# Seven block products per weight pair: another order of the products in gate and up, and another place for one of their PSUM tiles

## The chip, the cores and the metric

The kernel runs on one core of one Trainium2 chip. The metric is the device time of one execution in microseconds (us); lower is better. Engines are called by the names of the profile: PE (TensorE matmul), PEld (its weight load), DVE (VectorE), ACT (ScalarE), POOL (GpSimd), SP (SyncE, which here issues the loads).

## The reference

A trunk of two layers on 512 tokens with 1024 features: a gated short convolution first, then dilated attention, and behind each of them the same feed-forward block. The change lies in that block alone, in the two products `gate` and `up` (1024 features in, 2816 out, each):

```python
def swiglu(x, w_gate_up, w_down):
    g, u = jnp.split(x @ w_gate_up, 2, axis=-1)
    return (jax.nn.silu(g) * u) @ w_down

# once per layer:
f = swiglu(rms_norm(h, ffn_norm_pre[layer]), ffn_w_gate_up[layer], ffn_w_down[layer])
h = h + rms_norm(f, ffn_norm_post[layer])
```

All of it is float32. The kernel keeps each operand as a high part and a low part and adds three matmuls (high x high, low weights x high, high x low) for every block.

## The kernel before

**The stage.** `ffn` (L512) works through the gate and up columns in chunks of 256. Chunks 0 and 1 go through ordinary products. Chunks 2 to 10 (L543) go through the class `Pair` (L395): for each chunk one pair object for the gate columns, then one for the up columns, so 18 pairs per layer and 36 in the program. In what follows pair m is the m-th of a layer, from 0; even pairs are gates, odd ones are ups.

**One pair** multiplies 256 columns of weights (two blocks `n1`, `n2` of 128 columns, each in two halves `k1`, `k2` of the 1024 input features) by 512 tokens, and does it with seven block products in place of eight, on sums of the weight blocks and on sums of the token blocks (`xs`, made once per layer). A block product (L429) is 12 matmuls of 128x256. They are issued through `strict` (L134), which ties every matmul behind the one traced before, so PE runs the products in exactly the order in which `ffn` calls p1 to p7.

**The weights of a pair** are made when the object is built (L404 to L422), ahead of its first product: `a1` is the split of `n1` (ACT casts the high part, L94, DVE subtracts for the low part, L95); `dh` and `dl` (called `a22`) are the split of one quarter of the raw weights; then four additions on DVE (L407) overwrite the raw weights in place; then `s1` and `s2` are the splits of the two sums. Products 1 and 2 read `a1`, 6 and 3 read `s1`, 7 and 5 read `s2`, 4 reads `dh` and `dl`. `dh` and `dl` lie in the tag "ah" of the pool `apool`, which has 4 buffers: room for two pairs. `a1`, `s1` and `s2` share a tag of 6 buffers, the raw weights have 2.

**The results.** Three PSUM tiles per pair: `z` takes products 1, 6, 7 and 4 one after the other, each added onto the sum so far; `zx` takes product 2; `zy` takes 5 and later 3. PSUM has two tags, "mm" and "at", of 4 banks each. After each product on `z` the sum so far is read out before the next may be added: ACT copies it after p1 (L440) and after p6 (L448) and negates it after p7 (L455); after p4 ACT (gate, L471) or DVE (up, L473) reads it. DVE adds `zx` after p2 (L444), `zy` after p3 (L478); `c22` (L458 and L462 or L464) finishes the block that needs p7 and p5. p4 and p3 of a pair are held back and run between products of the next pair (`before` in L542 to L568).

**Everything else** on ACT, DVE and SP is placed by the tile planner when the program is built, instruction by instruction into one fixed queue per engine; a tile whose buffer is taken waits until the last reader of the tile before it is done. After the last pair the stage `down` (L343) follows, whose matmuls aren't tied to the order of the products.

Of the kernel before, what the change touches and what calls it, by code (L numbers as in the profile page):

```python
# [38 lines left out]
def trunk(  # L39
# [49 lines left out]
    def bank(tag, name):  # L89
        return psum.tile([P, T], F32, tag=tag, name=name)  # L90

    def split(hi, lo, src):

        return [nc.scalar.copy(hi, src).ins,  # L94
                nc.vector.tensor_tensor(lo, src, hi.bitcast(F32), ALU.subtract).ins]  # L95
# [9 lines left out]
    def parts(src, gain=None, pool=wp, bufs=6):  # L105


        _, a, b = src.shape
        w = pool.tile([P, 2 * a, b], F32R, tag="w", name="w", bufs=bufs, align_bytes=LINE)
        wh, wl = w[:, 0:a], w[:, a:2 * a]  # L110
        if gain is None:
            split(wh, wl, src)
            return wh, wl
        for i in range(a):
            g = gain[:, i:i + 1]
            nc.scalar.mul(wh[:, i], src[:, i], g)  # L116
            nc.vector.scalar_tensor_tensor(  # L117
                wl[:, i], src[:, i], g, wh[:, i].bitcast(F32), ALU.mult, ALU.subtract)
        return wh, wl
# [5 lines left out]
    def load_cols(w, c0):  # L125

        return load(w[:, c0:c0 + 256].rearrange("(k p) n -> p k n", p=P), KT, 256)
# [70 lines left out]
    def makers(tag, raw, gain=None, fused=True):  # L198

        ws = []  # L200

        def make(j):
            cs = slice(j * P, (j + 1) * P)
            ps = bank(tag, tag + "f")
            if gain is not None and not fused:
                for k in range(0, KT, 4):
                    g = gain[:, k:k + 4].rearrange("p (a x) -> p a x", x=1)
                    nc.vector.tensor_tensor(raw[:, k:k + 4, cs], raw[:, k:k + 4, cs],
                                            g.broadcast_to([P, 4, P]), ALU.mult)
            if gain is None or not fused:  # L210
                w = parts(raw[:, :, cs])
                return ps, lambda low, k: w[low][:, k, :]
            if not ws:
                ws.extend(gained(raw, gain))
            return ps, lambda low, k: ws[k // 4][low][:, k % 4, cs]

        return [lambda j=j: make(j) for j in range(2)]
# [76 lines left out]
    class Next:  # L294
# [3 lines left out]
        def __init__(self, pool, ys, gpost, gpre, n=0):  # L298
            self.pool, self.ys, self.n = pool, ys, n
            self.gpost, self.gpre = (g if g is None else row_gain(pool, g) for g in (gpost, gpre))  # L300
            self.hn, self.ssq, self.yg = {}, {}, {}
            self.marks, self.added, self.normed, self.made = {}, {}, {}, {}
# [92 lines left out]
    class Pair:  # L395
# [5 lines left out]
        def __init__(self, pool, raw, xs, gate, act):  # L401
            self.pool, self.xs, self.gate, self.act = pool, xs, gate, act
            n1, n2 = raw[:, :, 0:P], raw[:, :, P:2 * P]
            k1, k2 = slice(0, KT // 2), slice(KT // 2, KT)  # L404

            def add(out, a, b):
                nc.vector.tensor_tensor(out, a, b, ALU.add)  # L407

            a1 = parts(n1)
            a22 = [pool.tile([P, KT // 2, P], F32R, tag="ah", name=n, align_bytes=LINE)  # L410
                   for n in ("dh", "dl")]
            split(*a22, n2[:, k2])
            add(n2[:, k2], n2[:, k1], n2[:, k2])
            add(n2[:, k1], n1[:, k1], n2[:, k1])
            add(n1[:, k1], n1[:, k1], n2[:, k2])
            add(n1[:, k2], n1[:, k2], n1[:, k1])
            s1 = parts(n1)
            s2 = parts(n2)
            self.w = {
                1: [z[:, k1] for z in a1], 2: [z[:, k2] for z in a1],  # L420
                6: [z[:, k1] for z in s1], 3: [z[:, k2] for z in s1],
                7: [z[:, k1] for z in s2], 5: [z[:, k2] for z in s2], 4: a22}  # L422

            self.z, self.x, self.y = (bank(t, n)[:, 0:T // 2] for t, n in (
                ("mm", "z"), ("mm", "zx"), ("at", "zy")))
            self.r = pool.tile([P, T], F32, tag="al", name="r", align_bytes=LINE)
            self.r2 = pool.tile([P, T], F32, tag="al", name="r2", align_bytes=LINE)[:, 0:T // 2]

# [83 lines left out]
    def ffn(layer, pending, norms, after):  # L512
        w = ffn_w_gate_up[layer]
        with ExitStack() as phase:
            apool = phase.enter_context(tc.tile_pool(name=f"a{layer}", bufs=4))
            act = []
            for n, bufs in ((1, NF // 2 - 6), (0, 6)):
                actp = tc.tile_pool(name=f"act{layer}{n}", bufs=1)
                stack = phase.enter_context(ExitStack())
                pool = stack.enter_context(actp)  # L520
                act = [pool.tile([P, 2 * T], F32, tag=f"act{k}", name="act")
                       for k in range(bufs)] + act

            def loads(c):
                return [load_cols(w, c0 + c * 256) for c0 in (0, DFF)]

            for c in range(2):
                rg, ru = loads(c)
                mg, mu = makers("mm", rg), makers("at", ru)
                rest = pending.rest() if c == 0 else {}  # L530
                if c == 1:
                    rest["marks"] = [pending.made[NT - 1]] * 4
                ps = feature_mms([mg[0], mu[0], mg[1], mu[1]], **rest)
                for j in range(2):
                    s = apool.tile([P, T], F32, tag="silu", name="s", bufs=2)
                    nc.scalar.activation(s, ps[2 * j], AF.Silu)
                    nc.vector.tensor_tensor(
                        act[c][:, j * T:(j + 1) * T], ps[2 * j + 1], s, ALU.mult)
            norms.close()
            with tc.tile_pool(name=f"sums{layer}", bufs=1, side="right") as sums:  # L540
                xs = sums_of_x(sums, act[-4:])
                before = None  # L542
                for c in range(2, NF // 2):  # L543
                    gate = None
                    for raw in loads(c):
                        p = Pair(apool, raw, xs, gate, act[c])
                        p.p1()
                        if gate and c == NF // 2 - 1:
                            before.p4()
                            p.p6()  # L550
                            before.p3()
                            p.p7()
                            p.p2()
                            p.p5()
                            p.c22()
                            p.p4()
                            p.p3()
                            break
                        p.p2()
                        if before:  # L560
                            before.p4()
                        p.p6()
                        if before:
                            before.p3()
                        p.p5()
                        p.p7()
                        p.c22()
                        before = gate = p  # L568
            npool = norm_pool(norms, f"{layer}f")

            def held_pool():

                stack.close()
                return stack.enter_context(tc.tile_pool(name=f"held{layer}", bufs=2))

            halves = [a[:, j * T:(j + 1) * T] for a in act for j in range(2)]
            return down(apool, halves, ffn_w_down[layer], held_pool, lambda ys: after(npool, ys))

    def norm_pool(stack, n):

        return stack.enter_context(tc.tile_pool(name=f"norm{n}", bufs=2, side="right"))
# [3 lines left out]
    with ExitStack() as phase:  # L585
# [57 lines left out]
        for c in range(KT // 2):  # L643
# [56 lines left out]
            lambda: phase.enter_context(tc.tile_pool(name="heldc", bufs=2)),  # L700
            lambda ys: Next(npool, ys, mix_norm_post[0], ffn_norm_pre[0]))
    pending = ffn(0, pending, norm0, lambda pool, ys: Next(pool, ys, ffn_norm_post[0], None))


# [300 lines left out]
    with ExitStack() as phase:  # L1005
# [22 lines left out]
        class Last(Next):  # L1028
# [3 lines left out]
            def after_half(self, tt, n):  # L1032
                self.add(tt, n)
                if n == 1:
                    for q, c in zip((nc.sync, nc.scalar if tt == NT - 1 else nc.sync, nc.sync),
                                    self.pieces(tt)):
                        q.dma_start(out[0, tt * P:(tt + 1) * P, c], h[:, tt, c])

        ffn(1, pending, norm1, lambda pool, ys: Last(pool, ys, ffn_norm_post[1], None))


# [43 lines left out]
```

## Time and profile before

| | |
|---|---|
| time, median of 3 runs | 1454.47 us (1453.3 to 1454.65) |
| the profiled execution's own time | 1453.27 us |
| its span, first to last instruction | 1451.5 us |
| PE busy | 1433.4 us, 99% of the span |
| PEld / DVE / ACT / POOL busy | 1286.6 / 913.6 / 760.4 / 59.7 us |
| granted TensorE clock, mean | 0.997 |
| matmuls of the pairs (lines z, zx, zy of the page's part 5) | 864 + 432 + 432 in the lines shown, and those of p4 |

The busy time of PE is made of matmul records that overlap: a 128x256 matmul is recorded with 284 ns, while the next one starts 120 ns later. Progress is therefore read from starts, not from durations. A row of a timeline merges neighbouring instructions of one kind and gives the start, the time from the first start to the last end, and how many they are; a bracket says how long the engine was idle ahead of it and what ended that.

### The profile page before, as it was taken

Reading aid. Unit: us, or ns where it says so; the run is one execution under the profiler, and the core shown is the slowest. Engines: PE = TensorE matmul, PEld = TensorE weight load, DVE = VectorE, ACT = ScalarE, POOL = GpSimd, SP = SyncE. Lnnn points to the kernel's source line nnn. Section 1 sums busy time; section 2 is a strip of 40 time slices with the busy share of each in tenths; the row PEclk is TensorE's granted clock in tenths of the full one; section 3 lists DMA queues with packets and bytes.
Section 4 is the critical chain, followed back from the end, with each engine's and each line's share of the span. In section 5 each row is a group of like instructions: output and inputs, shape, how many; then the busy total and the mean of one; then the engine's idle time right before and its main releaser. Section 6 shows DMA issues by size and latency. Waiting matters only on the chain.

```text
span 1451.5 us, 23433 instructions
## 1 busy us (share of the span) xinstructions
PE 1433.4 (99%) x9456; PEld 1286.6 (89%) x9456; DVE 913.6 (63%) x1747; ACT 760.4 (52%) x1543; POOL 59.7 (4%) x108
## 2 busy tenths in 40 slices
PE   9999999999999999999999999999999999999998
PEld 7888898999988889898899889889789999998886
DVE  5644577888864456757457555755539688886433
ACT  5322344445443336896777778668544445454321
POOL 1000110000000010010000001000011000000000
PEclk9999999999999999999999999999999999999999
DMA  6333213232342402323212322321112232334311
GB/s 220 116 116 104 71 59 117 88 117 93 112 160 89 143 30 88 116 62 100 92 44 89 103 72 61 103 72 60 60 59 94 81 117 88 117 113 146 105 58 58
DMA packets 110530, 137.65 MB, mean 95 GB/s; under 512 B 3501, under 2 KB 99285, under 8 KB 110422
## 3 DMA queue, kind: packets, MB, share of 16 engines
q1 hardware_dynamic: 108852, 135.69, 28.2%
q8 instruction: 74, 1.21, 0.4%
q0 software_dynamic: 1280, 0.26, 0.3%
q14 instruction: 34, 0.28, 0.1%
q10 hardware_dynamic: 290, 0.20, 0.0%
HBM read 133.92 MB, written 2.23 MB: 94 GB/s over the span
## 4 chain that ended last, share of the span: by engine, by line
PE 95%; issue 2%; ACT 1%; DVE 1%; POOL 1%; POOLq 0%; DVEq 0%; ACTq 0%
PE mmf L134 17%; PE z L134 14%; PE vps L134 10%; PE atf L161 10%; PE zy L134 7%; PE mmf L161 7%; PE zx L134 4%; PE s L134 2%; PE o L134 2%; PE tr L134 2%; PE y L134 1%; PE tr L284 1%; PE y0a L230 1%; PE y1b L232 1%; PE y0a L232 1%
## 5 line engine op out<-in xcount | busy, mean ns | idle before, releaser
L95 DVE TENSOR_TENSOR w<-raw,w 128x1024 fp32r<-128x1024 f32 x212 | 251.6, 1220 | 81.7 <-ACT w L94 81.4
L94 ACT CAST w<-raw 128x1024 fp32r<-128x1024 f32 x212 | 212.7, 1046 | 107.3 <-PE atf L161 43.1
L134 PE MATMUL mmf<-x,w 128*128 128x512 f32 x1056 | 246.5, 391 | 0.0
L134 PEld LDWEIGHTS mmf<-x,w 128*128 128x128 f32 x1056 | 196.2, 188 | 39.4
L117 DVE SCALAR_TENSOR_TENSOR w<-raw,cols,w 128x256 fp32r<-128x256 f32 x272 | 115.4, 479 | 103.8 <-ACT w L116 103.8
L161 PE MATMUL atf<-x,w 128*128 128x512 f32 (+1 forms) x816 | 174.7, 340 | 0.0
L161 PEld LDWEIGHTS atf<-x,w 128*128 128x128 f32 x816 | 134.9, 190 | 16.8
L116 ACT ACTIVATE w<-raw,cols 128x256 fp32r<-128x256 f32 x272 | 115.1, 499 | 63.4 <-PE mmf L134 46.4
L134 PE MATMUL vps<-w,x 128*128 128x256 f32 x1152 | 142.3, 284 | 0.0
L134 PEld LDWEIGHTS vps<-w,x 128*128 128x128 f32 x1152 | 139.0, 192 | 1.9
L161 PE MATMUL mmf<-x,w 128*128 128x256 f32 (+1 forms) x624 | 131.3, 326 | 1.0 <-ACT x L94 0.6
L134 PE MATMUL z<-xs,w 128*128 128x256 f32 x864 | 115.8, 284 | 4.0 <-ACT r L440 4.0
L134 PEld LDWEIGHTS z<-xs,w 128*128 128x128 f32 x864 | 108.8, 192 | 4.6 <-ACT r L440 4.4
L161 PEld LDWEIGHTS mmf<-x,w 128*128 128x128 f32 x624 | 99.3, 191 | 11.5 <-ACT x L94 1.3
L407 DVE TENSOR_TENSOR raw<-raw 128x512 f32<-128x512 f32 x144 | 98.4, 688 | 2.9
L95 DVE TENSOR_TENSOR al<-act,ah 128x512 fp32r<-128x512 f32 x44 | 30.0, 690 | 90.1 <-ACT ah L94 90.0
L94 ACT CAST ah<-act 128x512 fp32r<-128x512 f32 x44 | 26.9, 620 | 110.2 <-PE y3b L230 101.7
L758 ACT COPY sw<-mmf 32x512 f32<-32x512 f32 x92 | 53.2, 578 | 30.1 <-PE mmf L134 18.8
L831 ACT ACTIVATE p<-p,nm 128x256 f32<-128x256 f32 (+1 forms) x128 | 61.5, 482 | 9.8 <-DVE nm L828 9.7
L760 DVE TENSOR_TENSOR qk<-mmf,cos 128x512 f32<-128x512 f32 x46 | 31.8, 690 | 46.4 <-ACT sw L759 46.3
L134 PE MATMUL zy<-xs,w 128*128 128x256 f32 x432 | 57.7, 283 | 0.0
L134 PE MATMUL zx<-x,w 128*128 128x256 f32 x432 | 57.7, 283 | 0.0
(220 smaller groups left out, 2403.7 us busy)
## 6 DMA issues: line engine op xcount, KB each, us to landing
raw<-in_ffn_w_gate_up SPq DMA_DIRECT2D x44, 1024.0 KB, 5.1
raw<-in_w_kv SPq DMA_DIRECT2D x24, 1024.0 KB, 5.2
raw<-in_ffn_w_down SPq DMA_DIRECT2D x22, 1024.0 KB, 4.9
raw<-in_w_q SPq DMA_DIRECT2D x12, 1024.0 KB, 5.0
raw<-in_conv_w_in SPq DMA_DIRECT2D x11, 1024.0 KB, 5.3
raw<-in_conv_w_out SPq DMA_DIRECT2D x4, 1024.0 KB, 4.9
raw<-in_w_o SPq DMA_DIRECT2D x4, 1024.0 KB, 5.1
h<-in_x SPq DMA_DIRECT2D x4, 512.0 KB, 7.3
```

The costliest lines, as they stand in the source:

```text
L94: return [nc.scalar.copy(hi, src).ins, nc.vector.tensor_tensor(lo, src, hi.bitcast(F32), ALU.subtract).ins]
L95: nc.vector.tensor_tensor(lo, src, hi.bitcast(F32), ALU.subtract).ins]
L116: nc.scalar.mul(wh[:, i], src[:, i], g)
L117: nc.vector.scalar_tensor_tensor(wl[:, i], src[:, i], g, wh[:, i].bitcast(F32), ALU.mult, ALU.subtract)
L134: traced[:] = [op(*args, **kwargs).ins]
L161: nc.tensor.matmul(*args, **kwargs)
L230: nc.tensor.matmul(o, ah, wl[i], start=False, stop=False)
L232: mm = nc.tensor.matmul(o, al, wh[i], start=False, stop=last)
L407: nc.vector.tensor_tensor(out, a, b, ALU.add)
L758: nc.scalar.copy(w[s:s + 32], y[s + 32:s + 64])
L760: nc.vector.tensor_tensor(d, y, co, ALU.mult)
L831: nc.scalar.activation(p, p, AF.Exp, bias=nm[:, b:b + 1], scale=0.125, accum_out=st[:, b, hh, 1:2])
```

## The change

Two edits in `Pair` and `ffn`. `zx` moves from the PSUM tag "mm" to "at", so that "mm" serves one tile per pair and "at" two. And the products come in another order. With n for the pair being built and b for the pair before it, the order from the second pair on was

p1(n), p2(n), p4(b), p6(n), p3(b), p5(n), p7(n), and c22(n) behind it;

it becomes

p1(n), p7(b), and c22(b) behind it, p2(n), p5(n), p6(n), p4(b), p3(b).

The last pair of a layer has its own order: p1, p4(b), p6, p3(b), p7, p2, p5, c22, p4, p3 becomes p1, p7(b), c22(b), p2, p6, p4(b), p5, p7, c22, p3(b), p4, p3. The number of products, matmuls, copies, additions, splits and loads stays as it was.

```diff
             self.z, self.x, self.y = (bank(t, n)[:, 0:T // 2] for t, n in (
-                ("mm", "z"), ("mm", "zx"), ("at", "zy")))
+                ("mm", "z"), ("at", "zx"), ("at", "zy")))
...
                         p.p1()
                         if gate and c == NF // 2 - 1:
+                            before.p7()
+                            before.c22()
+                            p.p2()
+                            p.p6()
                             before.p4()
-                            p.p6()
+                            p.p5()
+                            p.p7()
+                            p.c22()
                             before.p3()
-                            p.p7()
-                            p.p2()
-                            p.p5()
-                            p.c22()
                             p.p4()
                             p.p3()
                             break
+                        if before:
+                            before.p7()
+                            before.c22()
                         p.p2()
+                        p.p5()
+                        p.p6()
                         if before:
                             before.p4()
-                        p.p6()
-                        if before:
                             before.p3()
-                        p.p5()
-                        p.p7()
-                        p.c22()
                         before = gate = p
```

## Rows read from the trace of the kernel before

**Rows 1.** Waits of PE over the whole span: us, times, longest.
```profile
PE z L134 <- ACT r L440: 4.0, 2, 2.0
```

**Rows 2.** ACT's and PE's timelines at the last pair of the first layer.
```profile
409.20 3.87 ACT L94 CAST w<-raw 128x1024 fp32r<-128x1024 f32 x4
...
413.29 0.36 ACT L440 COPY r<-z 128x256 f32<-128x256 f32 x1
...
413.70 1.70 PE L134 MATMUL z<-xs,w 128*128 128x256 f32 x12 [2.01 <-ACT r L440]
```

**Rows 3.** Windows: us; busy PE, PEld, DVE, ACT, POOL; clock; DMA; GB/s.
```profile
257.46:267.54 10.08, 10.08 (x87) 10.08 (x85) 9.13 (x14) 3.58 (x7) 0.00 (x0) 1.00 0.31 104
267.54:277.62 10.08, 10.08 (x87) 10.08 (x85) 7.86 (x11) 6.54 (x11) 0.00 (x0) 1.00 0.32 106
```

**Rows 4.** PE's timeline from pair 2's p1 on (p1, p6, p3, p5, p7, p6).
```profile
257.46 1.60 PE L134 MATMUL z<-x,w 128*128 128x256 f32 x12
...
261.78 1.60 PE L134 MATMUL z<-xs,w 128*128 128x256 f32 x12
263.22 1.60 PE L134 MATMUL zy<-x,w 128*128 128x256 f32 x12
264.66 1.60 PE L134 MATMUL zy<-xs,w 128*128 128x256 f32 x12
266.10 1.60 PE L134 MATMUL z<-xs,w 128*128 128x256 f32 x12
...
271.86 1.60 PE L134 MATMUL z<-xs,w 128*128 128x256 f32 x12
```

**Rows 5.** Tile dh: what ended idle time before its instructions; us, times.
```profile
  PE z L134: 37.3, 31
```

**Rows 6.** ACT's timeline, weights of pairs 3 and 4.
```profile
261.86 0.62 ACT L94 CAST dh<-raw 128x512 fp32r<-128x512 f32 x1 [1.81 <-PE z L134]
...
267.80 0.39 ACT L455 ACTIVATE r<-z 128x256 f32<-128x256 f32 x1 [4.01 <-PE z L134]
268.08 2.94 ACT L94 CAST w<-raw 128x1024 fp32r<-128x1024 f32 x3
...
271.94 0.62 ACT L94 CAST dh<-raw 128x512 fp32r<-128x512 f32 x1 [0.35 <-PE z L134]
...
276.78 2.95 ACT L94 CAST w<-raw 128x1024 fp32r<-128x1024 f32 x3 [0.75 <-DVE raw L407]
```

**Rows 7.** DVE's timeline, weights of pair 3 and, from 272.56 on, of pair 4.
```profile
262.65 0.69 DVE L95 TENSOR_TENSOR dl<-raw,dh 128x512 fp32r<-128x512 f32 x1
263.37 1.42 DVE L407 TENSOR_TENSOR raw<-raw 128x512 f32<-128x512 f32 x2
...
265.80 0.68 DVE L484 TENSOR_TENSOR act<-r,s 128x512 f32<-128x512 f32 x1
266.40 0.69 DVE L407 TENSOR_TENSOR raw<-raw 128x512 f32<-128x512 f32 x1
...
269.15 3.50 DVE L95 TENSOR_TENSOR w<-raw,w 128x1024 fp32r<-128x1024 f32 x3 [0.51 <-ACT w L94]
272.56 0.42 DVE L444 TENSOR_TENSOR r<-zx,r 128x256 f32<-128x256 f32 x1
272.90 0.68 DVE L95 TENSOR_TENSOR dl<-raw,dh 128x512 fp32r<-128x512 f32 x1
273.61 1.42 DVE L407 TENSOR_TENSOR raw<-raw 128x512 f32<-128x512 f32 x2
...
275.28 1.41 DVE L407 TENSOR_TENSOR raw<-raw 128x512 f32<-128x512 f32 x2
277.86 3.50 DVE L95 TENSOR_TENSOR w<-raw,w 128x1024 fp32r<-128x1024 f32 x3 [1.17 <-ACT w L94]
```

**Rows 8.** Page, part 5: busy us, mean ns of one; idle before, releaser.
```profile
L95 DVE TENSOR_TENSOR w<-raw,w 128x1024 fp32r<-128x1024 f32 x212 | 251.6, 1220 | 81.7 <-ACT w L94 81.4
```

**Rows 9.** Window around the stall of rows 2; columns as in rows 3.
```profile
409.00:415.00 6.00, 3.99 (x34) 3.79 (x32) 5.06 (x5) 5.96 (x10) 0.00 (x0) 1.00 0.21 46
```

## The prediction

> **What bounds the kernel now.** I read the list of PE's waits first, then timelines and windows of the stage that the change touches. In the whole span PE waited for a copy of `z` only twice, 2.0 us each [rows 1]: once per layer, ahead of p6 of the last pair [rows 2]. In the two periods shown PE was busy for all of the 10.08 us [rows 3], and its seven products start 1.44 us apart (261.78, 263.22, 264.66, 266.10 in [rows 4]). So two products between two on one bank already hide the copies everywhere but at the end. PE is the bound of the stage; DVE comes next with 9.13 and 7.86 us of 10.08 [rows 3], and the reader should keep that closeness in mind.
>
> The second thing to see is how the weights of a pair are made, because the new order moves the products that release their buffers. `dh` and `dl` have room for two pairs, so the cast `dh` of pair m must wait for p4 of pair m-2, its last reader. The trace shows that this wait is real: idle time ahead of `dh` was ended by PE's `z` 31 times, 37.3 us in all [rows 5] (32 are to be expected, pairs 2 to 17 of two layers), and `dh` starts 0.08 us after p4 ends: 261.86 after 261.78, 271.94 after 271.86 [rows 4, 6]. Behind `dh` hangs everything else: `dl`, then four additions that overwrite the raw weights, then the casts and subtractions of `s1` and `s2`.
>
> **How long that chain is.** Let R be the end of p4 of pair m-2, the moment at which p6 starts in [rows 4].
> Pair 4, a gate, R = 271.86: `dh` 271.94, `dl` 272.90, additions 273.61 to 276.69 (275.28 + 1.41), casts from 276.78, subtractions from 277.86 [rows 6, 7]. The three subtractions are `s1`, `s2` and `a1` of the next pair, in the order in which the code makes them; one lasts 1.22 [rows 8], so they start (3.50 - 1.22) / 2 = 1.14 apart and `s2` is done at 277.86 + 1.14 + 1.22 = 280.22, R + 8.36. In this, `dl` waited about 0.3 us for the addition L444, which in the new order does not fall there: 8.06.
> Pair 3, an up, R = 261.78: L484 stands between the additions, they end at 267.09, the casts start only at 268.08 behind L455, and `s2` is done at 269.15 + 2.36 = 271.51, R + 9.73 [rows 6, 7]. Without the wait for L455 it would be 267.09 + 3.53 (0.09 to the cast, 1.08 to the subtraction, 2.36, all as in pair 4) = R + 8.84, and less 0.14 by which `dl` was late, R + 8.70.
>
> **The change part by part.**
> *What the chain is given.* Before, behind p4(m-2) come p6, p3, p5, p7, p1(m), p2(m), p4 and then p6(m), which needs `s1`: 7 products, 10.08 us. p5(m), which needs `s2`, comes two later: 12.96. The chain of 7.2 to 9.7 fits, and nothing waits. After, behind p4(m-2) come p3(m-2), p1(m), p7(m-1), p2(m) and at once p5(m): 4 products, 5.76 us for `s2`, and 7.20 for `s1`. Three things work together: p4 comes later in its period, and p6 and p5 change places and come earlier behind it, while `s2` is still made last.
> *The wait it adds.* The new reading of L455 falls near the cast (p7 ends at R + 4.32) and may push a gate's casts by some 0.15, so I take 8.2 for gates and 8.7 for ups. p5 then starts 2.44 or 2.94 late; with some 0.05 us of hand-over, 2.5 and 3.0. Queued behind it on PE are p6, p4 and p3, since the products are tied. The loss is not caught up: the next R is p5, p6 and p4 behind (4.32), so the loop runs at 8.2 + 4.32 = 12.5 and 13.0 us per pair in place of 10.08. DVE has 12.5 us for its 8 to 9 and does not bind by its load; it binds by latency. Pairs 0 and 1 find empty buffers. Pairs 2 to 16 pay: 8 gates x 2.5 + 7 ups x 3.0 = 41.0 us per layer.
> *Low and high end.* If the planner made `s2` ahead of `s1`, the wait would shrink by 1.14, and if it also cast during the last additions, `s1` at p6 would bind: 8.2 - 7.2 = 1.0 and 1.5. In every period shown the casts come after all four additions, so I stay away from this end. If every pair stood behind L455 as pair 3 did, 9.73 - 5.76 = 4.0 per pair. p7 comes earlier relative to the casts now, so I stay away from that end too.
> *The end of the stage.* Pair 17 has p6 in the fourth place: `s1` is done at 8.70 - 1.14 = R + 7.56 against 5.76, a wait of 1.85. The wait for L440 that stood there, 2.01 with four casts of 3.87 us ahead of it in ACT's queue [rows 2], goes. Sum: -0.15 per layer. Between p7 and p4 only one product (1.44) is left to hide L455 (0.39); if four casts stood ahead of it, up to 3.87 - 1.44 = 2.4 us would be open, unless PE takes matmuls of `down`, which are not tied. I take 0.
> *The banks.* `zx` moves to "at": a bank now serves again after two pairs. `zy` of pair m-2 is read by L478 about 0.6 us after R + 1.44 and written again by p5(m) at R + 5.76 or later; `zx` is free much earlier. The cover is 3 us; without it the price would be one read of 0.42. I take nothing. Loads, copies and additions are unchanged in number; the loads gain time.
> *The rule for the change.* The copies of `z` cost 4.0 us in all [rows 1], so that is what spacing can win. The Trainium skill (Perfetto Trace Analysis, section Matmuls) says that independent matmul groups should rotate through PSUM banks, so that reading one out overlaps the next group. It speaks for this change; by it alone the time would be 4 us shorter, which is the first rival below.
>
> **Sum.** 2 x (41.0 - 0.15) = 81.7 us. The profiled execution took 1453.27: 1535.0. It lies 1.2 below the median of the runs, so the forecast is 1536 us.
>
> **Rivals.**
> *The copies were the cost and the chain is covered: 1450 us.* Place: p6 of pair 17; price 2 x 2.0 us, with nothing put in its place. It decides if `s2` can be done within 5.76 us of p4(m-2). For it: DVE idles about 1 us per period, and a planner that sees PE wait orders anew. Against: with no delay at all between its links the chain is `dh`, `dl`, four additions and two splits, 8.06 us, each link waiting for the one before. Chance 0.05.
> *`s2` ahead of `s1`, or casts during the additions:* 8 x 1.0 + 7 x 1.5 = 18.5 up to 8 x 1.3 + 7 x 1.8 + 0.9 = 24 us per layer, so 1491 to 1502. Chance 0.08.
> *Casts held behind a wait on ACT in all pairs:* 15 x 4.0 + 0.8 = 61 per layer, 1576; in half of them 1556. Chance 0.09.
> *The clock falls during the new pauses.* Around the pause of 2.01 us PE was busy for 3.99 of 6.00 us and the granted clock stayed at 1.00, the 2.4 GHz level [rows 9]; the new period is busier, 10.08 of 12.8. If one product behind each pause ran at 1.2 GHz, 1.44 more each, 30 x 1.44 = 43: 1579. Chance 0.02. The Trainium skill (TensorE: Matmul & The Clock Gate, section A second HAM failure mode: psum-queue depth-cycling) tells of a kernel whose short pauses between groups made the clock swing; no row here shows it.
> *Nothing measurable,* the gain at the end against small waits: 1454. Chance 0.02.
>
> **How the numbers follow.** The forecast has 0.74, with a range of its own of 1520 to 1552 (0.5 us per pair to either side). The 8-in-10 range is 1505 to 1570; left out are the gain, no change, the clock, `s2` first and the upper part of the held casts, 0.19 in all. Slower by over 0.2% (3 us, about what a measurement of this kernel can tell from no change): 0.93; within: 0.02; faster: 0.05.
>
> **What the profile of the changed kernel would show.** PE's waits should list `zy` (p5) waiting for DVE's L95 some 30 times, 2 to 3 us each, in both layers; the starts of p1 should be 12.5 to 13.0 us apart from pair 2 on; `dh` should still start 0.1 us behind p4; DVE's busy time should hardly change. I am wrong if p5 follows p2 without a gap, if the wait names ACT's copies, or if `s2` is ready within 5.76 us of p4.

## The result, and the profile after

The changed kernel takes 1608.44 us (median of 4 runs, 1606.55 to 1612.22) where the kernel before takes 1454.56: a ratio of 1.1062, with a 95% interval from 1.1049 to 1.1074. It is 154 us slower. The forecast was slower, by 82 us. The profiled execution took 1607.52 us, its span is 1605.7.

The page of the changed kernel, parts 1 and 2 (busy time, share of the span and instructions; then tenths in 40 slices):

```profile
span 1605.7 us, 23415 instructions
...
PE 1504.9 (94%) x9456; PEld 1345.5 (84%) x9456; DVE 920.5 (57%) x1747; ACT 768.3 (48%) x1543; POOL 59.9 (4%) x108
...
PE   9999998887889999999999999999999788888998
...
PEclk9999999988889999999999999999999888879999
```

The reader should see two things. PE's share fell from 99% to 94% in the slices of the two feed-forward blocks, so PE pauses there. And PE's busy time rose by 71 us although it has the same 9456 matmuls, in the slices in which the granted clock drops. Not all of the 71 us is clock: p4_one_earlier below, with the clock at 0.999, has 1442.8 us, 9.4 more than the kernel before; these are likely the tails of matmul records that a pause lays open. DVE's busy time hardly moved (913.6 to 920.5).

PE's waits in the changed kernel (us, times, longest), beside the one line of [rows 1]:

```profile
PE zy L134 <- ACT w L94: 45.9, 30, 2.1
PE zy L134 <- DVE w L95: 36.7, 30, 1.4
...
PE z L134 <- ACT w L94: 2.3, 2, 1.2
PE z L134 <- DVE w L95: 1.8, 2, 0.9
```

The two waits for L440 are gone. In their place p5 (`zy`) waits 30 times for the cast of `s2` and 30 times more for its subtraction, and p6 of the last pair (`z`) twice for `s1`. That is 86.7 us of listed waits, in the places that the prediction named.

PE's timeline of the changed kernel, p2, p5 and p6 of pair 3, and p5 and p6 of pair 5:

```profile
273.12 1.60 PE L134 MATMUL zx<-x,w 128*128 128x256 f32 x12
276.84 0.38 PE L134 MATMUL zy<-xs,w 128*128 128x256 f32 x1 [2.12 <-ACT w L94]
278.28 1.57 PE L134 MATMUL zy<-xs,w 128*128 128x256 f32 x11 [1.06 <-DVE w L95]
279.69 1.60 PE L134 MATMUL z<-xs,w 128*128 128x256 f32 x12
...
303.61 0.47 PE L134 MATMUL zy<-xs,w 128*128 128x256 f32 x1 [2.12 <-ACT w L94]
305.06 2.71 PE L134 MATMUL zy<-xs,w 128*128 128x256 f32 x11 [0.97 <-DVE w L95]
307.57 2.76 PE L134 MATMUL z<-xs,w 128*128 128x256 f32 x12
```

The first matmul of p5 needs only the high part, the second the low part too, so the one pause is listed in two; the prediction had expected one line, DVE's L95. The list counts idle time from the end of a record and so counts too little: pair 3's pause is listed with 2.12 + 1.06 = 3.18 us and makes its period 3.69 us longer (next windows). Pair 5 shows what was not forecast: the 11 matmuls that need 1.41 us from their start to p6 at 278.28 need 2.51 us at 305.06. The windows of three periods of the same kernel, from one p7 to the next (columns as in [rows 3]):

```profile
271.68:285.45 13.77, 10.59 (x86) 10.19 (x85) 8.51 (x13) 6.03 (x10) 0.00 (x0) 1.00 0.24 77
285.45:298.45 13.00, 10.60 (x86) 10.20 (x85) 8.92 (x14) 4.60 (x7) 0.00 (x0) 1.00 0.27 82
298.45:312.67 14.22, 11.12 (x70) 10.63 (x69) 6.79 (x10) 5.30 (x9) 0.00 (x0) 0.76 0.23 74
```

Where the clock stays at 2.4 GHz, a period is 13.0 us with a gate's pause and 13.8 with an up's, in place of 10.08 [rows 3]; 12.5 and 13.0 were forecast. In the third window the clock was at its lower level, 1.2 GHz, for part of the time.

### The profile page after: what moved, and what is told of

It reads as the page before. It is cut to its first block, busy times and chain, and to the rows that moved or that the text cites. A ratio compares the mean times of both kernels' runs of the same rounds, so it can differ in the third digit from the quotient of the medians.

```text
span 1605.7 us, 23415 instructions
## 1 busy us (share of the span) xinstructions
PE 1504.9 (94%) x9456; PEld 1345.5 (84%) x9456; DVE 920.5 (57%) x1747; ACT 768.3 (48%) x1543; POOL 59.9 (4%) x108
## 4 chain that ended last, share of the span: by engine, by line
PE 88%; DVE 6%; issue 2%; ACT 2%; POOL 1%; POOLq 0%; DVEq 0%; ACTq 0%
PE mmf L134 15%; PE z L134 15%; PE vps L134 9%; PE atf L161 9%; PE zy L134 8%; PE mmf L161 6%; DVE w L95 4%; PE s L134 2%; PE o L134 2%; PE tr L134 2%; PE zx L134 2%; ACT w L94 1%; PE y L134 1%; PE tr L284 1%; PE y0b L228 1%
## 5 line engine op out<-in xcount | busy, mean ns | idle before, releaser
L95 DVE TENSOR_TENSOR w<-raw,w 128x1024 fp32r<-128x1024 f32 x212 | 251.5, 1220 | 72.8 <-ACT w L94 72.5
L134 PE MATMUL zy<-xs,w 128*128 128x256 f32 x432 | 95.6, 381 | 82.6 <-ACT w L94 45.9
L134 PEld LDWEIGHTS zy<-xs,w 128*128 128x128 f32 x432 | 80.1, 271 | 95.1 <-ACT w L94 52.0
L134 PE MATMUL z<-xs,w 128*128 128x256 f32 x864 | 142.8, 326 | 4.1 <-ACT w L94 2.3
L134 PEld LDWEIGHTS z<-xs,w 128*128 128x128 f32 x864 | 136.8, 238 | 4.9 <-ACT w L94 2.8
L448 ACT COPY r<-z 128x256 f32<-128x256 f32 x36 | 13.4, 373 | 175.6 <-PE z L134 175.6
L95 DVE TENSOR_TENSOR al<-act,ah 128x512 fp32r<-128x512 f32 x44 | 30.2, 690 | 92.7 <-ACT ah L94 92.7
L95 DVE TENSOR_TENSOR dl<-raw,dh 128x512 fp32r<-128x512 f32 x36 | 24.9, 692 | 99.4 <-ACT dh L94 97.7
```

The costliest lines, as they stand in the source:

```text
L134: traced[:] = [op(*args, **kwargs).ins]
L448: nc.scalar.copy(self.r[:, 256:512], self.z)
```

## The experiments

Ten kernels, each timed beside the kernel before on the same chip, in three groups; the kernel before took 1454.65, 1453.58 and 1453.82 us there. Three dots in an edit mark lines left out.

### A third set of dh and dl

Of the changed kernel; every third pair keeps `dh` and `dl` in 4 KB of the token sums. The lines of `sums_of_x` that free this place aren't shown; through them product 6 reads the low part that belongs to product 5, so this kernel leaves out one low part and is an experiment only:

```diff
-            a22 = [pool.tile([P, KT // 2, P], F32R, tag="ah", name=n, align_bytes=LINE)
-                   for n in ("dh", "dl")]
+            a22 = home or [pool.tile([P, KT // 2, P], F32R, tag="ah", name=n, align_bytes=LINE)
+                           for n in ("dh", "dl")]
...
-                        p = Pair(apool, raw, xs, gate, act[c])
+                        m = 2 * c - 4 + (gate is not None)
+                        p = Pair(apool, raw, xs, gate, act[c], xs["a22"] if m % 3 == 2 else None)
```

> The changed kernel with room for a third set of dh and dl: every third pair keeps them in 4 KB that one low part of the token sums gave up (product 6 reads the low part of the token sum of product 5, so that part of the computation is changed; instructions and their number are the same). Theory A (p5 waits since dh must wait for p4 two pairs earlier, and the slow clock comes from these pauses): pauses gone, granted clock back at about 0.997, and without the two waits of 2.0 us for the copies about 1450 us. Theory B (the new order itself, or zx and zy in one PSUM tag, makes the matmuls slow; the pauses are a thing by themselves): the pauses go, the mean clock stays near 0.95, about 1608 - 83 = 1525 us. Theory C (another buffer or queue holds s2 back): nothing changes, 1608 us.

Measured: 1448.63 us, ratio to the kernel before 0.9962 (0.9949 to 0.9975). In a window of the first stage (columns as in [rows 3]) PE was busy without a break and the clock stayed up:

```profile
258.00:420.00 162.00, 162.00 (x1349) 161.87 (x1348) 130.13 (x196) 83.70 (x140) 0.00 (x0) 1.00 0.32 105
```

The order of the products and the number of matmuls are those of the changed kernel; with room for one more `dh` and `dl` all of the 160 us are gone. This is theory A. It also says that the new order without its side effect is 6.0 us faster than the old one, though PE's list still has one wait for L440 of 0.9 us.

### Unneeded matmuls in the pauses, 20 and 8 of them, and the same 20 without a pause

```diff
+        def filler(self, n):
+            for i in range(n):
+                strict(nc.tensor.matmul, self.spare, self.w[2][0][:, i % 4, :],
+                       self.xs[2][0][:, :, i % 4, :], start=True, stop=True,
+                       skip_group_check=True)
+
         def p5(self):
+            if self.spare is not None:
+                self.filler(20)
             self.product(self.y, 5, True, True)
...
```

> The changed kernel with 20 unneeded matmuls of 128x256 ahead of p5 in pairs 2 to 16 of each layer, into a spare PSUM bank that nothing reads: 2.4 us of work in a place where PE pauses 2.4 to 3.2 us. Theory A (pauses lower the clock): 600 matmuls more and yet faster, clock about 0.997, 1454.5 + 82.7 = about 1537 us. Theory B (slow matmuls have a cause of their own): not faster, 1608 us or, if the fillers are slow too, up to 1680 us.

Measured: 1554.14 us, 54.3 us less than without the 600 matmuls. PE's timeline at p5 of pair 3, and the windows of two periods:

```profile
273.03 2.56 PE L134 MATMUL spare<-x,w 128*128 128x256 f32 x20
275.43 0.28 PE L134 MATMUL zy<-xs,w 128*128 128x256 f32 x1
276.76 1.58 PE L134 MATMUL zy<-xs,w 128*128 128x256 f32 x11 [1.05 <-DVE w L95]
```

```profile
257.15:270.15 13.00, 12.73 (x106) 12.53 (x105) 8.91 (x14) 4.60 (x7) 0.00 (x0) 1.00 0.25 82
270.15:283.94 13.79, 12.74 (x106) 12.54 (x105) 8.53 (x13) 6.03 (x10) 0.00 (x0) 1.00 0.23 76
```

The periods are 13.00 and 13.79 us, the same as the undisturbed ones of the changed kernel: the fillers cost nothing, and `s2` comes no earlier. What they give back is the clock. So this run separates the two causes: pauses 1554.1 - 1448.6 = 105.5 us, clock 1608.4 - 1554.1 = 54.3 us. The split is good to a few us, since this run still loses some clock: behind the wait of pair 17, which has no fillers, the clock of the second layer was 0.66 and 0.77 in two windows of 3 us, some 1.7 us by estimate (3 x 0.34 + 3 x 0.23). The expected 1537 was missed by 17. It took the price of the pauses, 82.7, from PE's list, which counts too little, and left out pair 17; the clock came back as expected.

> The kernel before with the same 20 unneeded matmuls ahead of p5 in pairs 2 to 16: the price of the fillers where PE does not pause. Both theories: 30 x 20 x 0.12 = 72 us more, 1526 us, clock about 0.997. If it is much less, fillers overlap with something and fill_after says less.

Measured: 1520.54 us, 1.0455 (1.0440 to 1.0471), 65.9 us more than the kernel before. PE's timeline at the first fillers:

```profile
264.81 2.56 PE L134 MATMUL spare<-x,w 128*128 128x256 f32 x20
267.21 1.60 PE L134 MATMUL zy<-xs,w 128*128 128x256 f32 x12
```

Twenty fillers take 267.21 - 264.81 = 2.40 us, 0.12 each, so 72 us in all as expected. The 6.1 us that are missing are a gain elsewhere: PE's list of this run has no wait for L440 any more. That is the same size as the 6.0 us of third_set.

> As fill_after, with 8 unneeded matmuls in place of 20: 0.9 us of the pauses of 2.4 and 3.2 us are filled, 1.5 and 2.3 remain, about as long as those of p4_one_earlier (1.4 to 1.5, clock 0.999) and p6_first (2.05 in every second pair, clock 0.990). The fillers lie in the pause, so the periods without loss of clock stay at 13.0 and 13.8 us. Theory (the clock is lost only where a pause is long): 1554 to 1565 us, clock about 0.99. Rival (every pause that is left costs clock in proportion to its length): 54 us x (3.8 / 5.6) = 37 us above fill_after, 1590 us.

Measured: 1562.60 us, mean clock 0.990. The lines of p5 in its list of PE's waits:

```profile
PE zy L134 <- DVE w L95: 37.1, 30, 1.4
PE zy L134 <- ACT w L94: 16.5, 15, 1.2
```

53.6 us of pauses are left in place of 82.6, and the loss by the clock is 8.5 us in place of 54.3. The loss is not in proportion to the length of the pauses; it comes with the long ones. The trace of this run shows it one by one: in the pairs the clock drops seven times, each time within or right behind a pause listed with 2.0 us or more (an up's, 1.16 + 1.07, or pair 17's, 1.17 + 0.87). Nine such pauses bring no drop, and none comes with a gate's shorter one.

### One edit alone: zx in the other PSUM tag

```diff
-                ("mm", "z"), ("mm", "zx"), ("at", "zy")))
+                ("mm", "z"), ("at", "zx"), ("at", "zy")))
```

> The kernel before with the first edit of the change alone: zx in the PSUM tag at, the order of the products as before. Theory A: 1454.5 us, within 1 us, since no bank was waited for. Theory B in its form with the banks (zx and zy in one tag make the matmuls of zy slow): some 70 us more, 1525 us, with a lower clock or longer matmuls of zy.

Measured: 1453.72 us, 0.9998 (0.9989 to 1.0008). With the old order the bank has no price and no gain. Its trace shows one thing more, at the wait of [rows 2], which this kernel still has in both layers; PE's rows, two windows of the first layer and one of the second:

```profile
414.40 2.17 PE L134 MATMUL z<-xs,w 128*128 128x256 f32 x12 [2.01 <-ACT r L440]
...
1317.12 1.70 PE L134 MATMUL z<-xs,w 128*128 128x256 f32 x12 [2.01 <-ACT r L440]
```

```profile
411.00:414.00 3.00, 1.39 (x12) 1.19 (x10) 3.00 (x3) 3.00 (x5) 0.00 (x0) 1.00 0.00 0
414.00:417.00 3.00, 2.60 (x15) 2.60 (x16) 1.60 (x2) 2.03 (x6) 0.00 (x0) 0.73 0.84 273
...
1317.00:1320.00 3.00, 2.88 (x24) 2.88 (x25) 1.32 (x2) 1.75 (x5) 0.00 (x0) 1.00 0.85 265
```

The same pause of 2.01 us that left the clock alone in the kernel before [rows 9] is followed by a lower clock in the first layer here, and by the full clock in the second layer of the same execution. So the edit of the bank alone does not decide it; what does stays open.

### p4 earlier, by two places and by one

```diff
                         p.p2()
+                        if before:
+                            before.p4()
                         p.p5()
                         p.p6()
                         if before:
-                            before.p4()
                             before.p3()
```

> The changed order with p4 of the pair before two places earlier: p1, p7(b), p2, p4(b), p5, p6, p3(b); the end of the stage as in the change. Behind p4 there are now 7 products (10.08 us) ahead of the p5 that needs s2, where the changed kernel's chain took 8.7 to 9.4. Theory A (the chain from p4 to s2): no pauses, clock 0.997, and as the waits at the end of the stage are gone too, 1449 us, like third_set. Rival (p7 to p4 has only p2 between now, so the negating copy L455 is waited for): a pause of up to 1 us per pair, 1480 us or more.

Measured: 1448.40 us, 0.9962 (0.9950 to 0.9975), with no wait of `z` or `zy` in PE's list and the window of the first layer's stage full:

```profile
258.00:420.00 162.00, 162.00 (x1347) 161.78 (x1346) 140.33 (x200) 83.59 (x142) 0.00 (x0) 1.00 0.35 114
```

The wait for L455 that the rival saw does not come up. This kernel is 5.2 us faster than the kernel before and level with third_set, without leaving anything out, so it is the version to keep. With p4 one place later than that:

```diff
                         p.p2()
                         p.p5()
+                        if before:
+                            before.p4()
                         p.p6()
                         if before:
-                            before.p4()
                             before.p3()
```

> The changed order with p4(b) one place earlier: p1, p7(b), p2, p5, p4(b), p6, p3(b). Five products (7.20 us) behind p4 for s2. Theory A: pauses of 8.66 - 7.20 = 1.5 (gates) and 9.43 - 7.20 = 2.2 us (ups), 8 x 1.5 + 7 x 2.2 = 27 us per layer, 1503 us if the clock holds under the shorter pauses, up to 1555 us if it falls as in the changed kernel. Rival (pauses have nothing to do with p4): as the changed kernel, 1608 us, or no pauses at all.

Measured: 1504.50 us, 1.0348 (1.0334 to 1.0362), mean clock 0.999. PE's timeline, p5 of two pairs in a row:

```profile
274.09 1.57 PE L134 MATMUL zy<-xs,w 128*128 128x256 f32 x11 [1.39 <-DVE w L95]
...
285.95 1.58 PE L134 MATMUL zy<-xs,w 128*128 128x256 f32 x11 [1.53 <-DVE w L95]
...
297.97 1.58 PE L134 MATMUL zy<-xs,w 128*128 128x256 f32 x11 [1.39 <-DVE w L95]
```

The place of p4 sets the size of the pause: 7 products behind it none, 5 products 1.4 to 1.5 us per pair in the list, 4 products (the change) 2.4 to 3.2. It does so product by product, for two periods take 297.97 - 274.09 = 23.88 us here and 13.77 + 13.00 = 26.77 in the changed kernel, 2.89 apart, which is two products. Only the sum came as expected; the pauses of gates and ups are nearly equal here, where 1.5 and 2.2 were expected.

### The other two parts of the loop: p6 ahead of p5, and s2 made first

```diff
-                        p.p5()
                         p.p6()
+                        p.p5()
```

> The changed order with p6 ahead of p5 again, as before the change; p4 stays late. Now p6 needs s1 at 5.76 us behind p4, and s1 is done 1.14 ahead of s2. Theory A: the wait moves from p5 to p6 and shrinks by 1.14, to 1.8 (gates) and 2.5 us (ups), 32 us per layer, 1512 us if the clock holds, up to 1565 us if it falls. Rival (p5 next to p2 is what is slow): the pauses go, 1450 us.

Measured: 1525.85 us, 1.0498 (1.0483 to 1.0512), mean clock 0.990. The waits moved from `zy` to `z`, as expected, and are listed with 1.2 us for gates and 2.05 for ups. The second kernel only swaps two lines in which weights are made:

```diff
-            s1 = parts(n1)
             s2 = parts(n2)
+            s1 = parts(n1)
```

> The changed kernel with s2 made ahead of s1, nothing else. Theory A: p5 waits 1.14 less, 1.8 and 2.5 us, and p6 behind it does not wait for s1: 1512 us if the clock holds, up to 1565 us if it falls. If s2 is cast while the last additions run (they do not touch its half of the raw weights), the wait shrinks further, to about 1 us, and the time to 1480 us.

Measured: 1481.32 us, 1.0186 (1.0171 to 1.0202), mean clock 0.996. ACT's timeline (first row) and DVE's show for one pair why it is at the low end:

```profile
269.16 1.05 ACT L94 CAST w<-raw 128x1024 fp32r<-128x1024 f32 x1 [0.39 <-DVE raw L407]
...
268.44 2.14 DVE L407 TENSOR_TENSOR raw<-raw 128x512 f32<-128x512 f32 x3
270.49 1.22 DVE L95 TENSOR_TENSOR w<-raw,w 128x1024 fp32r<-128x1024 f32 x1
```

The cast of `s2` starts at 269.16, while the additions run until 270.58: with `s2` first the planner does overlap them. With `s1` first it does not, since `s1` needs the last addition and stands ahead.

### Another end alone

```diff
                             before.p4()
-                            p.p6()
                             before.p3()
-                            p.p7()
+                            p.p6()
                             p.p2()
+                            p.p7()
                             p.p5()
```

> The kernel before with another order in the last pair alone: p1, p4(b), p3(b), p6, p2, p7, p5, c22, p4, p3, so two products in place of one stand between p1 and p6. Theory (the gain of third_set and p4_two_earlier is the wait for L440 at the end of the stage): the wait of 2.01 us shrinks by one product, 1.44 us, in both layers: 2.9 us, 1451.5 us. Rival (p7 to p4 has one product less, and L455 stands behind casts): the wait moves there, 1454 us or more.

Measured: 1450.32 us, 0.9973 (0.9963 to 0.9983), 3.5 us less than the kernel before. The wait ahead of p6 in PE's timeline is what the subtraction gave, 2.01 - 1.44:

```profile
413.45 1.70 PE L134 MATMUL z<-xs,w 128*128 128x256 f32 x12 [0.57 <-ACT r L440]
```

## Why the prediction was right and wrong

**Right: which wait, where, and how many.** The step "What the chain is given" held, and third_set and the two places of p4 show it as the cause. `dh` of pair m still starts 0.08 us behind p4 of pair m-2, p5 waits 30 times, p6 of pair 17 twice. The relation "pause = chain - 5.76" holds to 0.02 us. The changed kernel's DVE and ACT, with R = 268.80, the end of p4:

```profile
269.53 0.69 DVE L95 TENSOR_TENSOR dl<-raw,dh 128x512 fp32r<-128x512 f32 x1
270.44 0.42 DVE L478 TENSOR_TENSOR r<-zy,r 128x256 f32<-128x256 f32 x1 [0.22 <-PE zy L134]
270.78 0.68 DVE L407 TENSOR_TENSOR raw<-raw 128x512 f32<-128x512 f32 x1
271.38 0.68 DVE L484 TENSOR_TENSOR act<-r,s 128x512 f32<-128x512 f32 x1
271.99 1.41 DVE L407 TENSOR_TENSOR raw<-raw 128x512 f32<-128x512 f32 x2
273.74 0.42 DVE L458 TENSOR_TENSOR r<-r,zy 128x256 f32<-128x256 f32 x1 [0.34 <-ACT r L455]
274.08 0.68 DVE L407 TENSOR_TENSOR raw<-raw 128x512 f32<-128x512 f32 x1
274.76 0.42 DVE L444 TENSOR_TENSOR r<-zx,r 128x256 f32<-128x256 f32 x1
275.87 3.50 DVE L95 TENSOR_TENSOR w<-raw,w 128x1024 fp32r<-128x1024 f32 x3 [0.69 <-ACT w L94]
```

```profile
274.79 2.94 ACT L94 CAST w<-raw 128x1024 fp32r<-128x1024 f32 x3 [0.18 <-DVE raw L407]
```

`s2` is done at 275.87 + 2.36 = 278.23, R + 9.43, and 9.43 - 5.76 = 3.67; the period is 13.77 - 10.08 = 3.69 longer. For a gate, with R = 282.57 and subtractions from 288.87 (rows below), it is 8.66 and 2.90, against 2.92 measured.

**Wrong in size: the chain of 8.2 and 8.7.** It measured 8.66 and 9.43. The additions were taken over from [rows 7] with what stood between them there. In the new order other readings fall into the same 5 us. In an up, L478 now stands ahead of the first addition and waits for p3 (0.22), and L458 stands ahead of the fourth and waits for L455 (0.34, and 0.33 of its own). I had put L455 near the casts of a gate and priced it at 0.15; L458 behind it on DVE I let fall into a gap. The ups end nearer to the rival of the held casts (4.0 per pair) than to the forecast (3.0). In a gate L478 delays the additions too, and three readings stand between them and the subtractions:

```profile
284.56 2.86 DVE L407 TENSOR_TENSOR raw<-raw 128x512 f32<-128x512 f32 x4
287.57 0.42 DVE L458 TENSOR_TENSOR r<-r,zy 128x256 f32<-128x256 f32 x1 [0.16 <-ACT r L455]
288.03 0.43 DVE L464 TENSOR_TENSOR act<-r,s 128x256 f32<-128x256 f32 x1
288.53 0.42 DVE L444 TENSOR_TENSOR r<-zx,r 128x256 f32<-128x256 f32 x1
288.87 3.48 DVE L95 TENSOR_TENSOR w<-raw,w 128x1024 fp32r<-128x1024 f32 x3
```

```profile
287.45 2.94 ACT L94 CAST w<-raw 128x1024 fp32r<-128x1024 f32 x3
```

The subtractions start 1.42 us behind the casts where I had 1.08. I had taken 0.3 us off the gates' chain because L444 would no longer fall on it; it does, ahead of the subtractions. Eight gates at 2.92 and seven ups at 3.69 are 49.2 us per layer where 41.0 was forecast. With the waits of pair 17 (4.1 listed; 1.85 per layer was forecast) that is 102.5 of the 105.5 us; of the 3 us left, 1.7 would be the clock that fill_after itself still lost.

**Wrong by its chance: the clock.** "The clock falls during the new pauses" stood among the rivals with 43 us and a chance of 0.02; it cost 54.3 us. This is what carried the time out of the range: with the longer chain alone it ends at 1554 us, inside it. The step that failed is the reading of [rows 9]: one pause, in one execution, without loss, and from it that the busier new period would be safe. The run with the one bank edit shows the same pause followed by a lower clock, and the changed kernel's windows have 1.00 and 0.76 in neighbouring periods. Which of the pauses bring the clock down stays open. The Trainium skill (TensorE: Matmul & The Clock Gate, section A second HAM failure mode: psum-queue depth-cycling) tells of another kernel, one that cycles through PSUM banks, in which short and frequent idle times of PE between matmul groups make the clock swing between its two levels. The swing agrees with the changed kernel's trace, 1.00 and 0.76; its pauses come from a weight buffer and not from PSUM. The mean clock gives the same order of size: 1605.7 x 0.046 = 74 us against 4 before, part of it while PE stood idle anyway.

**Right: the end and the bank.** The two waits of 2.0 us went, and the edit of the bank cost nothing. The order alone is worth 5 to 6 us (1448.4 and 1448.6), a little over the 4.0 of [rows 1]. Part of the rest is that the list counts too little: from the start of p4's last matmul to that of p6 (411.42 to 413.70, less the usual 0.12) such a pause costs 2.16 us. Clock lost behind those pauses can be another part, as bank_only's first layer shows it, but not in the profiled execution of the kernel before, where the clock was 1.00 behind both; how much it is stays open. The gain is small against what the order costs in buffers, 105.5 us of pauses and 54.3 of clock. The Trainium skill (Perfetto Trace Analysis, section Matmuls) says that independent matmul groups should rotate through PSUM banks, so that reading one out overlaps the next group. The trace agrees: with more products between two on one bank the 4.0 us of waits for the copies are gone from PE's list of the changed kernel.

**The sum, as the runs give it:** 1454.6 - 6.0 (order without side effects) + 105.5 (pauses) + 54.3 (clock) = 1608.4. The low end that I priced for `s2` ahead of `s1`, 1.0 to 1.5 us per pair, was on record as unlikely for the change, and is about what s2_first shows when the two lines are swapped: (1481.3 - 1448.6) / 30 = 1.1, with pair 17's waits in it.

## What to carry to other kernels

When products are moved, count for every buffer they read how much work lies between its last reader and the next product that needs its successor: here 12.96 us became 5.76, against a chain that needs 9. Readings that are moved with the products fall between the links of that chain; price them by the new neighbours, not by the old rows. And where pauses like these, 2 us and more, come back in every period, price PE's clock as well: one pause without a loss is no evidence that the next has none.

## What the runs showed of the hardware

Filling the pauses with 600 matmuls that nobody reads made the kernel 54.3 us faster, with the same periods as those in which the clock had not dropped; the mean granted clock went from 0.954 to 0.995. In the profiled executions listed pauses of 1.4 to 1.5 us in every pair (p4_one_earlier) left the mean clock at 0.999, 1.2 and 2.05 us in turn (p6_first) at 0.990, and 2.4 and 3.2 us in turn (the change) at 0.954. And the same pause of 2.01 us was followed by a window at 0.73 in one layer of bank_only and by 1.00 in the other.
